# Adaptive average pooling: the last store issued by GpSimd instead of ScalarE

## The chip, the core and the metric

The kernel runs on one core of a Trainium2 chip. A core has five engines, each with an instruction queue of its own: TensorE (unused here), VectorE (DVE in the profile), ScalarE (ACT), GpSimd (POOL) and SyncE (SP). Sixteen DMA engines move data between the chip's main memory (DRAM) and the on-chip memory of 128 partitions. The metric is the device time of one execution in microseconds (us); lower is better.

## The reference

The input is x of shape 32 x 256 x 4096 in float32, the output has 256 values for each of the 8192 rows. Since 4096 / 256 = 16, every output is the mean of 16 neighbouring inputs:

```python
for i in range(output_size):
    start = int(i * length / output_size)
    end = int((i + 1) * length / output_size)
    result[:, :, i] = np.mean(x[:, :, start:end], axis=-1)
```

134.22 MB are read and 8.39 MB written, and each input is used once.

## The kernel before

The 8192 rows are taken as 16 tiles of 128 partitions by 4 rows, 64 KB for each partition and 8.39 MB in all. Fifteen tiles are loaded whole (L81, issued by SP) into two buffers named `xin` that take turns. The sixteenth tile is loaded in two halves (L89). All loads stand in SP's queue, and a load waits until the tile that used its buffer before has been reduced.

`pooled` (L62) reduces a tile. GpSimd adds the two halves of each window for the second half of the tile's windows, in place (L66). VectorE sums the windows of the first half, 16 wide (L69), and then the windows that GpSimd has shortened to 8 (L70). ScalarE multiplies the sums by 1/16 (L73). For the fifteen whole tiles the result goes into `res_many`, 60 KB for each partition, which stays on the chip until the end. For the sixteenth it goes into `res_last`, 4 KB for each partition.

There are three stores. All are issued by ScalarE, through the helper `store` (L57): `res_many` in one piece of 7680 KB once the fifteenth tile is done, and `res_last` after both of its halves, in two pieces of 120 and of 8 partitions (480 KB and 32 KB). The helper adds the name of each store to `tc.no_tile_sem_insts`, so that the closing code which the framework writes does not wait for the landing, and lets the store raise the semaphore `stored` by 16 when its data has landed.

The end of the program is written in this order. `tc.compile()` (L102) adds the closing code: every engine runs a DRAIN and signals, GpSimd gathers the signals and releases all, then GpSimd clears the framework's semaphores, and a second round of DRAIN, gathering and release follows. After that SP alone waits until `stored` is 48, three stores of 16 (L103), and clears it (L104); the profile shows the wait and the clear as one instruction on L104.

Of the kernel before, what the change touches and what calls it, by code (L numbers as in the profile page):

```python
# [1 line left out]

# [4 lines left out]


@with_exitstack
def kernel(  # L10
    ctx: ExitStack,
    tc: tile.TileContext,
    x: bass.AP,
    output_size: int,
    out: bass.AP,
):

    nc = tc.nc
    F32 = mybir.dt.float32
    X = mybir.AxisListType.X

    batch, channels, length = x.shape
    ob, oc, olen = out.shape
    assert ob == batch and oc == channels and olen == output_size
    assert length % output_size == 0
    window = length // output_size  # L30
    hw = window // 2
    inv_w = 1.0 / float(window)

    P = nc.NUM_PARTITIONS
    R = 4
    rows = batch * channels
    assert rows % (P * R) == 0
    ntiles = rows // (P * R)
    many = (ntiles - 1) * R
    cells = R * output_size  # L40
    m = cells // 2
    cols = R * length

    xr = x.rearrange("b c l -> (b c) l")
    orow = out.rearrange("b c o -> (b c) o")
    x_many = xr[0 : P * many, :].rearrange("(p r) l -> p (r l)", p=P, r=many)
    o_many = orow[0 : P * many, :].rearrange("(p r) o -> p (r o)", p=P, r=many)
    x_last = xr[P * many :, :].rearrange("(p r) l -> p (r l)", p=P, r=R)
    o_last = orow[P * many :, :].rearrange("(p r) o -> p (r o)", p=P, r=R)

    res_many = nc.alloc_sbuf_tensor("res_many", [P, (ntiles - 1) * cells], F32, align_bytes=256)
    res_last = nc.alloc_sbuf_tensor("res_last", [P, cells], F32, align_bytes=256)
    inpool = ctx.enter_context(tc.tile_pool(name="inpool", bufs=2))

    stored = nc.alloc_semaphore("stored")

    def store(out, in_):  # L57
        ins = nc.scalar.dma_start(out=out, in_=in_)
        tc.no_tile_sem_insts.add(ins.ins.name)
        ins.then_inc(stored, 16)  # L60

    def pooled(xin, res, base, n):  # L62


        k = n // 2
        nc.gpsimd.tensor_add(  # L66
            out=xin[:, k:n, 0:hw], in0=xin[:, k:n, 0:hw], in1=xin[:, k:n, hw:window]
        )
        nc.vector.reduce_sum(out=res[:, base : base + k], in_=xin[:, 0:k, :], axis=X)  # L69
        nc.vector.reduce_sum(  # L70
            out=res[:, base + k : base + n], in_=xin[:, k:n, 0:hw], axis=X
        )
        nc.scalar.mul(  # L73
            out=res[:, base : base + n], in_=res[:, base : base + n], mul=inv_w
        )

    for t in range(ntiles - 1):
        xbuf = inpool.tile([P, cols], F32, name="xin")
        if t == 1:
            nc.vector.memset(xbuf[:, 0:1536], 0.0)  # L80
        nc.sync.dma_start(out=xbuf, in_=x_many[:, t * cols : (t + 1) * cols])  # L81
        pooled(xbuf.rearrange("p (o w) -> p o w", w=window), res_many, t * cells, cells)

    half = cols // 2
    xbuf = inpool.tile([P, cols], F32, name="xin")
    for h in range(2):
        nc.sync.dma_start(  # L89
            out=xbuf[:, h * half : (h + 1) * half],  # L90
            in_=x_last[:, h * half : (h + 1) * half],
        )
    store(o_many, res_many[:, :])
    for h in range(2):
        xin = xbuf[:, h * half : (h + 1) * half].rearrange("p (o w) -> p o w", w=window)
        pooled(xin, res_last, h * m, m)
    for lo, hi in ((0, 120), (120, P)):
        store(o_last[lo:hi, :], res_last[lo:hi, :])

    ctx.pop_all().close()  # L100
    tc.close()
    tc.compile()  # L102
    nc.sync.wait_ge(stored, 48)  # L103
    nc.sync.sem_clear(stored)  # L104


# [1 line left out]
_INS = ['x', 'output_size']  # L108
_OUTS = [((32, 256, 256), 'float32')]

_NUMBERS = {'output_size': 256}


# [26 lines left out]
```

## Time and profile before

| | us |
|---|---|
| median of 3 runs (333.38 to 333.53) | 333.52 |
| the profiled execution's own time | 333.36 |
| its span, first to last instruction | 332.1 |
| DVE busy | 211.1 |
| POOL busy | 139.9 |
| ACT busy | 18.4 |

The profiled execution's time is 1.26 us more than its span, for what lies around the instructions. In the rows of the profile, q1 is the queue of DMAs that SP issues and q10 the queue of those that ACT issues. A name such as SPq or POOLq means the instruction queue of an engine: waits, DRAINs and issues of DMAs, none of which count as busy time. An issue of a DMA is short; its packets move later, on the sixteen DMA engines.

### The profile page before, as it was taken

What the parts mean: (1) busy time and instruction counts of PE and PEld (TensorE: products, weight loads), DVE (VectorE), ACT (ScalarE), POOL (GpSimd) and SP (SyncE); (2) the same over time, 40 slices, a digit from 0 to 9 for tenths busy, and PEclk for the clock granted to TensorE, in tenths of its full rate; (3) what the DMA queues carried; (4) which work ended last, traced back from release to release, by engine and by line L of the source; (5) the groups of instructions that cost most, each with busy time, mean ns of one, the idle gap of its engine ahead of it and who ended that gap; (6) DMA issues with size and microseconds to landing.
All of it is one profiled execution on the core that took longest, in us unless ns stands there. A gap on an engine that the chain in (4) does not pass through costs nothing.

```text
span 332.1 us, 167 instructions
## 1 busy us (share of the span) xinstructions
DVE 211.1 (64%) x35; ACT 18.4 (6%) x18; POOL 139.9 (42%) x21
## 2 busy tenths in 40 slices
DVE  1029396592939669293966929396693929569770
ACT  1000101001010100101010010101000010100100
POOL 0028091542809154270916427090642709068050
DMA  9898999989898998989899998989899898989997
GB/s 379 379 497 387 482 403 411 474 379 505 379 497 387 458 426 379 505 379 497 387 482 403 395 489 379 505 379 497 387 450 434 379 505 379 497 383 430 442 466 307
DMA packets 2743, 142.61 MB, mean 429 GB/s; under 512 B 311, under 2 KB 311, under 8 KB 439
## 3 DMA queue, kind: packets, MB, share of 16 engines
q1 hardware_dynamic: 2448, 134.22, 93.6%
q10 hardware_dynamic: 295, 8.39, 5.9%
HBM read 134.22 MB, written 8.39 MB: 429 GB/s over the span
## 4 chain that ended last, share of the span: by engine, by line
DMA 62%; POOL 20%; DVE 10%; issue 3%; POOLq 1%; ACT 0%
DMA xin<-in_x_dram 62%; POOL xin L66 20%; DVE res_many L70 9%; POOLq L102 1%; DVE res_last L70 1%; DVE xin L80 0%; ACT res_last L73 0%; POOLq L66 0%
## 5 line engine op out<-in xcount | busy, mean ns | idle before, releaser
L66 POOL TENSOR_TENSOR xin<-xin 128x4096 f32<-128x4096 f32 (+1 forms) x17 | 139.7, 8216 | 179.7 <-DMA xin<-in_x_dram 179.7
L69 DVE TENSOR_REDUCE res_many<-xin 128x512 f32<-128x8192 f32 x15 | 130.3, 8686 | 105.2 <-DMA xin<-in_x_dram 105.2
L70 DVE TENSOR_REDUCE res_many<-xin 128x512 f32<-128x4096 f32 x15 | 66.3, 4419 | 2.4 <-POOL xin L66 2.3
L73 ACT ACTIVATE res_many<-res_many 128x1024 f32<-128x1024 f32 x15 | 15.8, 1056 | 289.9 <-DVE res_many L70 289.9
L69 DVE TENSOR_REDUCE res_last<-xin 128x256 f32<-128x4096 f32 x2 | 8.8, 4414 | 2.1 <-DMA xin<-in_x_dram 2.1
L70 DVE TENSOR_REDUCE res_last<-xin 128x256 f32<-128x2048 f32 x2 | 4.6, 2280 | 0.1
L80 DVE MEMSET xin<- 128x1536 f32 x1 | 1.3, 1338 | 1.1 <-PEq L121 1.1
L73 ACT ACTIVATE res_last<-res_last 128x512 f32<-128x512 f32 x2 | 1.3, 629 | 13.7 <-DVE res_last L70 13.7
L73 ACT ACT_TABLE_LOAD x1 | 1.3, 1283 | 0.7 <-PEq L121 0.7
L121 POOL MEMSET const-float32-0.0<- 128x1 f32 x1 | 0.1, 98 | 0.2 <-issue 0.2
L121 POOL MEMSET const-bfloat16-1.0<- 128x1 bf16 x1 | 0.1, 101 | 0.0
L121 POOL MEMSET const-uint8-127<- 128x1 uint8 x1 | 0.1, 101 | 0.0
L121 POOL MEMSET const-float32-1.0<- 128x1 f32 x1 | 0.1, 98 | 0.0
## 6 DMA issues: line engine op xcount, KB each, us to landing
xin<-in_x_dram SPq DMA_DIRECT2D x2, 4096.0 KB, 21.6
out_dram<-res_many ACTq DMA_DIRECT2D x1, 7680.0 KB
out_dram<-res_last ACTq DMA_DIRECT2D x1, 480.0 KB
xin<-in_x_dram SPq DMA_DIRECT2D x15, 25.3
out_dram<-res_last ACTq DMA_DIRECT2D x1, 32.0 KB
```

Of the source, the lines that this page charges most:

```text
L66: nc.gpsimd.tensor_add(out=xin[:, k:n, 0:hw], in0=xin[:, k:n, 0:hw], in1=xin[:, k:n, hw:window])
L69: nc.vector.reduce_sum(out=res[:, base : base + k], in_=xin[:, 0:k, :], axis=X)
L70: nc.vector.reduce_sum(out=res[:, base + k : base + n], in_=xin[:, k:n, 0:hw], axis=X)
L73: nc.scalar.mul(out=res[:, base : base + n], in_=res[:, base : base + n], mul=inv_w)
L80: nc.vector.memset(xbuf[:, 0:1536], 0.0)
L102: tc.compile()
L121: nc = _bacc.Bacc("TRN2", target_bir_lowering=False, num_devices=1)
```

## The change

`store` gets the queue and the semaphore as arguments. The store of `res_many` stays with ScalarE and `stored`. The two stores of `res_last` are issued by GpSimd, after its own last work, and raise a new semaphore `stored_last`. At the end SP waits for 16 on `stored`, clears it, waits for 32 on `stored_last` and clears that.

```diff
     stored = nc.alloc_semaphore("stored")
+    stored_last = nc.alloc_semaphore("stored_last")
 
-    def store(out, in_):
-        ins = nc.scalar.dma_start(out=out, in_=in_)
+    def store(queue, sem, out, in_):
+        ins = queue.dma_start(out=out, in_=in_)
         tc.no_tile_sem_insts.add(ins.ins.name)
-        ins.then_inc(stored, 16)
+        ins.then_inc(sem, 16)
...
-    store(o_many, res_many[:, :])
+    store(nc.scalar, stored, o_many, res_many[:, :])
...
     for lo, hi in ((0, 120), (120, P)):
-        store(o_last[lo:hi, :], res_last[lo:hi, :])
+        store(nc.gpsimd, stored_last, o_last[lo:hi, :], res_last[lo:hi, :])
...
-    nc.sync.wait_ge(stored, 48)
+    nc.sync.wait_ge(stored, 16)
     nc.sync.sem_clear(stored)
+    nc.sync.wait_ge(stored_last, 32)
+    nc.sync.sem_clear(stored_last)
```

## The prediction, made before the changed kernel was run

> **What bounds the kernel now.** I read the page first, parts 1, 3 and 4.
>
> ```profile
> span 332.1 us, 167 instructions
> DVE 211.1 (64%) x35; ACT 18.4 (6%) x18; POOL 139.9 (42%) x21
> ...
> q1 hardware_dynamic: 2448, 134.22, 93.6%
> q10 hardware_dynamic: 295, 8.39, 5.9%
> HBM read 134.22 MB, written 8.39 MB: 429 GB/s over the span
> ```
>
> No engine is busy for more than 64%, while the packets of the two DMA queues fill 93.6 + 5.9 = 99.5% of the sixteen DMA engines' span. The kernel is bound by the bytes it moves. The change moves no byte less, so only the end can differ, where something may come after the last byte. The page's chain stops at the last multiply, so for the end I took the timeline of ACT from 300 us, and the waits of SP's queue.
>
> ```profile
> 306.69 1.06 ACT L73 ACTIVATE res_many<-res_many 128x1024 f32<-128x1024 f32 x1 [18.26 <-DVE res_many L70]
> 307.78 0.38 ACTq L58 DMA_DIRECT2D out_dram<-res_many  x1
> ...
> 322.12 0.63 ACT L73 ACTIVATE res_last<-res_last 128x512 f32<-128x512 f32 x1 [8.29 <-DVE res_last L70]
> 322.78 1.04 ACTq L58 DMA_DIRECT2D out_dram<-res_last  x2
> ...
> SPq L104 <- DMA out_dram<-res_last: 7.3, 1, 7.3
> ```
>
> The last multiply ends at 322.75, the two stores of `res_last` are issued from 322.78 to 323.82, and SP's last instruction waits 7.3 us for them, until 332.03. It is done at 332.06. What the 7.3 us are filled with is in the DMA view of three stretches, 314.1 to 315, 315 to 330 and 330 to 332.1 us, by the start of the packets:
>
> ```profile
> q10 hardware_dynamic: 16, 0.98, 251.9%
> q1 hardware_dynamic: 15, 0.00, 0.9%
> ...
> q10 hardware_dynamic: 96, 5.90, 90.7%
> ...
> DMA packets 167, 0.52 MB, mean 250 GB/s; under 512 B 39, under 2 KB 39, under 8 KB 167
> ```
>
> From 315 to 330 the engines do nothing but `res_many`: 96 packets in 0.907 x 15 x 16 = 217.7 engine-us, 2.27 us for each packet of 60 KB. Only then come the 128 packets of `res_last` and 39 small semaphore packets. The 8 or 9 data packets of an engine take about 1.4 us, and no packet starts after 331.6; the semaphore is full 0.43 us later. So `res_last`, issued at 323, has to queue until 330 anyway.
>
> The closing code is the last thing to read: L102 in narrow stretches around 324 us and the row of GpSimd's first DRAIN.
>
> ```profile
> L102 POOLq DRAIN  x1: 4556/4556/4556, 315.3 to 315.3; - x1
> ...
> L102 ACTq DRAIN  x1: 238/238/238, 323.9 to 323.9; - x1
> ...
> L102 SPq EVENT_SEMAPHORE  x1: 17/17/17, 324.7 to 324.7; - x1
> ```
>
> ACT's DRAIN (starting between 323.86 and 323.88) ends at 324.11, the last of the first round. SP's second release (starting between 324.73 and 324.75) ends at 324.76. The two rounds of gathering and release therefore take 0.65 us after the last DRAIN, all of it hidden under the 7.3 us in which `res_many` is still moving.
>
> **The change part by part.**
>
> *Taken off ACT.* Two issues, 1.04 us, and an ACT DRAIN that can be done about 1 us sooner. Nothing waits for that but the closing rounds, which have 7.3 us of cover: worth 0.
>
> *The wait on GpSimd.* The first store now waits in GpSimd's queue for the multiply at 322.75. GpSimd has had no work since its add ended at 319.77 (315.32 + 4.45). The hand-over costs 0.02 (DVE 322.10 to ACT 322.12) to 0.1 us. Behind the waiting store stand the second store, GpSimd's DRAIN and its gathering of the signals, and all engines wait for that gathering.
>
> *The issue on GpSimd.* No row shows one. From below there is ACT's issue of the same two stores, 0.43 to 0.58 us each (even 0.1 us, a GpSimd MEMSET, would gain nothing, since the DMA engines are taken until 330). From above there is GpSimd's longest single work nearby, 4.45 us each. I take 1 us each, near ACT's rows because the work is the same, more because another engine does it: issued by about 324.9. The first load, issued at 0.74, has its first packets after 1.72, so I add 1 us: 325.9. The cover is `res_many` until 330.02, so this costs 0. It would cost from an issue of the first store over 330.02 - 322.8 - 1.0 = 6.2 us on.
>
> *The transfer.* Same bytes, same engines, and a queue of its own. I expect the packets after those of `res_many`, or one of them between each two, since both give the same end. When `res_many` began (row of 314.1 to 315 above, and 16 q10 packets with 1 of q1 in the 2.25 us before), the load's sixteen semaphore packets on q1 were each let in after a single 60 KB packet of q10. So the engines seem to take turns packet by packet, and of the 8 packets for each engine at most 2 or 3 could slip in before `res_many` ends. All are done by 331.6 and landed by 332.02. Bounds: -0.15 us if the 9th packet of some engines finds a free one, +0.4 if the new queue's packets cost a quarter more. I take 0.
>
> *SP's end.* One wait and one clear more. SP's clear is 25 ns, and its closing instructions follow each other at 0.08 us (324.26, 324.35). After the closing code two of them cost 2 x (0.08 + 0.025) = 0.2 us if both semaphores are already full, where 0.04 us followed the landing before; if SP is already waiting, the second pair adds about 0.1.
>
> *GpSimd's DRAIN.* This decides. GpSimd's first DRAIN now stands behind its own two stores. Does it wait for their landing? The trace has a row on either side. ACT's DRAIN took 0.24 us, eight microseconds ahead of the landing of ACT's stores: by it the price is 0. GpSimd's DRAIN took 4.56 us, from 315.28 to 0.07 us after the add ended: by it a DRAIN of GpSimd is held by whatever GpSimd still owns. The nearest row for a GpSimd DRAIN is GpSimd's own, and the trace has one more hint: GpSimd's queue alone runs an INC_SWDGE_SEM at 0.1 us, by its name a count for DMAs, which no other queue shows. I take it that the DRAIN is held until `res_last` has landed. Then the closing rounds lose their cover and come behind the last byte:
>
> landing 332.02 + 0.07 (DRAIN) + 0.65 (two rounds) + 0.2 (SP) = 332.94, against 332.06 before: +0.88 us.
>
> The ends are 0.05 to 0.24 for the DRAIN, 0.6 to 0.7 for the rounds, 0.1 to 0.25 for SP and -0.15 to +0.4 for the transfer, together +0.56 to +1.55. The profiled execution would go from 333.36 to 334.24 and its span from 332.1 to 333.0; the runs' median is 0.16 above that execution, so 333.52 + 0.88 = 334.4.
>
> **The rivals.** 0.2% of 333.5 is 0.67 us, about what a measurement of this kernel can tell from no change.
>
> 1. *The DRAIN is not held* (the side of no change). It ends with the issue at about 325, the rounds at 325.7, under six more microseconds of cover, and only SP's second pair shows: +0.1 us, 333.6. For it: ACT's DRAIN. Against it: GpSimd's, 4.56 us. It decides unless GpSimd's DRAIN outlasts about 331.3, the landing less the rounds.
>
> 2. *Held, but `res_last` lands early.* If an engine gives the new queue one long turn, its 9 packets go after the `res_many` packet that runs at 325.9, by 328.2 + 1.4 = 329.6 at the latest, landed at 330.0, closing done at 330.8, still under `res_many`, which then lands at 332.0: +0.1 us, 333.6. The Trainium skill ("DMA: Bandwidth & Descriptors", Queues, rings and completion order) says so: an engine drains a whole packet, typically 9 to 17 descriptors, of one queue before it switches. By that rule the time would be 333.6; this trace speaks against it, with 16 q10 packets let in ahead of 15 of q1's.
>
> 3. *The issue is late.* With GpSimd's upper row, 4.45 us for each store, the second one is issued at 331.7 and moves from 332.7, landing at about 333.2, and with the DRAIN held the end is 334.1: +2.1 us, 335.6. Against it: ACT does the same in 0.5 us. The Trainium skill ("GPSIMD Engine Reference", Instruction dispatch) warns of about 6 us for the first call of freshly loaded code on GpSimd; as an estimate from it the packets would come at 322.8 + 6 + 2, 0.8 us after 330.02, and the time would be 335.2. No run here shows it for a DMA.
>
> 4. *Faster.* Were the packets spread evenly (-0.15) and the 0.43 us to the landing shared with `res_many`, the end could come 0.6 us sooner: 332.9. That is still inside 0.2%, and the packets' sum forbids more.
>
> **How the numbers follow.** Forecast 0.62; DRAIN not held 0.17; early landing 0.07; late issue 0.11; faster 0.03. Slower by over 0.2%: 0.58 of the forecast (its lowest ends fall below 0.67 us; I give them 0.04) + 0.11 = 0.69. Within 0.2%: 0.17 + 0.07 + 0.04 = 0.28. Faster by more needs something that I can't name: 0.03. The range reaches from 333.5, which takes in rivals 1 and 2 less the scatter of the runs, to 335.2, which takes in the forecast's own upper end (335.1) and part of rival 3. The forecast's own range is 334.1 to 335.1.
>
> **What would show it.** Right: a POOLq DRAIN on L102 several microseconds long, ending within 0.3 us of the last landing; the release on SP after it; SP's two clears at the very end, 0.7 to 0.9 us after the landing. The transfer step: still `res_many` alone until 330 and no packet of the new queue after 331.6. Wrong: GpSimd's DRAIN ending near 325 and SP waiting for `stored` at 331 (rival 1), the new queue's packets between 326 and 329 (rival 2), or a gap in the packets after 330 (rival 3).

## The result, and the profile after

The changed kernel takes 334.93 us (median of 4 runs, 334.89 to 335.0) against 333.52 us before (4 runs, 333.38 to 333.62): 1.41 us more, a ratio of 1.0043 with a 95% interval of 1.0029 to 1.0056. It is slower, as forecast, by more than the 0.88 us of the forecast and inside its range.

The page of the changed kernel shows the same work and the same bytes. GpSimd's row has two instructions and 1.2 us more, because the page counts GpSimd's issues of DMAs as work, which it does not do for ACT. GpSimd's queue appears as q0 with the kind software_dynamic:

```profile
span 333.2 us, 168 instructions
DVE 211.2 (63%) x35; ACT 18.4 (6%) x18; POOL 141.1 (42%) x23
...
q10 hardware_dynamic: 144, 7.86, 5.5%
q0 software_dynamic: 176, 0.52, 0.4%
```

The timeline of the end (start, duration, engine) shows GpSimd's two issues where ACT's stood, and the rows of the closing code (L104 here), in narrow stretches, show the DRAIN behind them. Columns of a row: count, shortest/median/longest in ns, first and last start.

```profile
322.08 0.63 ACT L74 ACTIVATE res_last<-res_last 128x512 f32<-128x512 f32 x1 [8.36 <-DVE res_last L71]
323.02 1.20 POOL L59 DMA_DIRECT2D out_dram<-res_last  x2 [3.29 <-ACT res_last L74]
...
L104 POOLq DRAIN  x1: 8947/8947/8947, 323.5 to 323.5; - x1
...
L104 SPq EVENT_SEMAPHORE  x1: 17/17/17, 333.0 to 333.0; - x1
...
L106 SPq EVENT_SEMAPHORE_RANGE_CLEAR  x1: 25/25/25, 333.1 to 333.1; - x1
...
L108 SPq EVENT_SEMAPHORE_RANGE_CLEAR  x1: 35/35/35, 333.2 to 333.2; - x1
```

The DRAIN on GpSimd starts at 323.46 and ends at 332.41. The last of the stores' semaphore increments in the trace is at 332.28. So the DRAIN was held until `res_last` had landed, and for 0.13 us more. (The row of the DRAIN starts before the second issue has ended, as that of before started just ahead of GpSimd's add; what counts is its end.) The release on SP, which stood at 324.74 before, is at 333.05, and SP's two clears end the program at 333.23. The row of SP's 7.3 us wait on L104 of before has no successor in the waits of SP's queue: when SP gets to its waits, both semaphores are full.

The stretches of the DMA view from 327.7 to 330 and from 331.6 on show the transfer:

```profile
q10 hardware_dynamic: 16, 0.98, 99.5%
q0 software_dynamic: 16, 0.06, 6.5%
...
DMA packets 17, 0.01 MB, mean 5 GB/s; under 512 B 15, under 2 KB 15, under 8 KB 17
```

While the sixteen last 60 KB packets of `res_many` start, sixteen packets of the new queue are let in, 0.06 MB: fifteen of 4 KB and one of a semaphore. The other 113 of 4 KB follow, and only 2 of them start after 331.6.

### The profile page after: what moved, and what is told of

The parts are those of the page before. It is cut to its first block, busy times and chain, and to the rows that moved or that the text cites. A ratio compares the mean times of both kernels' runs of the same rounds, so it can differ in the third digit from the quotient of the medians.

```text
span 333.2 us, 168 instructions
## 1 busy us (share of the span) xinstructions
DVE 211.2 (63%) x35; ACT 18.4 (6%) x18; POOL 141.1 (42%) x23
## 4 chain that ended last, share of the span: by engine, by line
DMA 66%; POOL 20%; DVE 10%; issue 1%; ACT 0%; POOLq 0%; SPq 0%
DMA xin<-in_x_dram 66%; POOL xin L67 20%; DVE res_many L71 9%; DVE res_last L71 1%; DVE xin L81 0%; POOL out_dram L59 0%; ACT res_last L74 0%; POOLq L104 0%; SPq L91 0%; POOLq L67 0%
## 5 line engine op out<-in xcount | busy, mean ns | idle before, releaser
L59 POOL DMA_DIRECT2D out_dram<-res_last x2 | 1.2, 606 | 3.3 <-ACT res_last L74 3.3
```

Source lines behind the costliest of these rows:

```text
L59: ins = queue.dma_start(out=out, in_=in_)
```

## The experiments

Two theories. **Cover**: GpSimd's DRAIN waits for the landing of GpSimd's own stores and so takes the closing code, and whatever else used to run under `res_many`, out of its cover. **Transfer** or **software queue**: the new queue's packets, or its use as such, cost the time. A smaller rival is the second **semaphore**. Medians are beside the kernel before on the same chip, 333.42 to 333.45 us.

**The semaphore alone.** ScalarE issues again, against the changed kernel:

```diff
-        store(nc.gpsimd, stored_last, o_last[lo:hi, :], res_last[lo:hi, :])
+        store(nc.scalar, stored_last, o_last[lo:hi, :], res_last[lo:hi, :])
```

> Only the second semaphore, with its wait and clear on SP; ScalarE issues all three stores as before. Theory 'cover' (the loss is GpSimd's DRAIN, which waits for the landing and pulls the closing code, and the other engines' end, behind it): +0.1 us against before, closing code at 324 us as before. Rival 'semaphore' (two waits and two clears at the end make the loss): +1.4 us as in the changed kernel. Rival 'transfer' (the packets of the software queue make the loss): +0.1 us.

333.43 us, ratio 0.9999 [0.9990, 1.0009]. The closing code's release is at 324.62 again. The second semaphore is not the cause.

**A queue of its own, but SP's.**

```diff
-        store(nc.gpsimd, stored_last, o_last[lo:hi, :], res_last[lo:hi, :])
+        store(nc.sync, stored_last, o_last[lo:hi, :], res_last[lo:hi, :])
```

> The stores of res_last in a queue of their own, but one that SP issues, with the own semaphore. Theory 'cover': SP's DRAIN is not held by a store of SP, as ACT's was not, so within 0.3 us of before (333.5 to 333.8). Rival 'transfer', in the form that any second queue beside res_many costs: about +1.4 us, 334.9.

333.52 us, ratio 1.0002 [0.9993, 1.0011]. The first packets of `res_last` go at 327.68, ahead of the end of `res_many` just as in the changed kernel. A second queue beside `res_many` costs nothing that can be measured. Nor is SP's DRAIN held by SP's own stores, whose last issue ends at 323.68 and which land at 332.05:

```profile
L104 SPq DRAIN  x2: 7/7/7, 324.0 to 324.1; - x2
```

**GpSimd's queue, used early.** GpSimd stores the first tile's results, ScalarE all else:

```diff
+        if t == 0:
+            store(nc.gpsimd, stored_last, o_many[:, 0:cells], res_many[:, 0:cells])
...
-    store(nc.scalar, stored, o_many, res_many[:, :])
+    store(nc.scalar, stored, o_many[:, cells:], res_many[:, cells:])
...
-        store(nc.gpsimd, stored_last, o_last[lo:hi, :], res_last[lo:hi, :])
+        store(nc.scalar, stored, o_last[lo:hi, :], res_last[lo:hi, :])
...
-    nc.sync.wait_ge(stored, 16)
+    nc.sync.wait_ge(stored, 48)
...
-    nc.sync.wait_ge(stored_last, 32)
+    nc.sync.wait_ge(stored_last, 16)
```

> GpSimd issues a 512 KB store with the own semaphore, but early: the first tile's part of res_many, after the first tile is scaled at about 37 us; ScalarE stores the other fourteen tiles and res_last at the end. Theory 'cover': the store has landed long before the end, GpSimd's closing DRAIN ends with its add at 320 us as before, so within 0.3 us of before. Rival 'software queue' (a program that uses GpSimd's queue pays for it at the end, wherever it is used): +0.4 to +1.4 us.

333.60 us, ratio 1.0004 [0.9996, 1.0013]. GpSimd's first DRAIN ends at 320.72, 0.16 us after its add. The use of the queue as such is not the cause.

**The wait for the landing, without GpSimd.** Against the kernel before:

```diff
-    stored = nc.alloc_semaphore("stored")
...
-        ins = nc.scalar.dma_start(out=out, in_=in_)
-        tc.no_tile_sem_insts.add(ins.ins.name)
-        ins.then_inc(stored, 16)
+        nc.scalar.dma_start(out=out, in_=in_)
...
-    nc.sync.wait_ge(stored, 48)
-    nc.sync.sem_clear(stored)
```

> All three stores issued by ScalarE as before, but the helper leaves the framework to wait for their landing ahead of its closing code; the semaphore stored and SP's wait and clear at the end fall away. No store of GpSimd at all. Theory 'cover': the closing rounds (0.65 us) and the 0.36 us that the changed kernel loses outside its span come behind the landing here too, less the clear: +0.8 to +1.2 us, 334.3 to 334.7. Rival 'transfer' or 'software queue': +0.0 to +0.1 us from the wait's place, at most the 0.65 us of the rounds with nothing outside the span.

334.85 us, ratio 1.0042 [1.0029, 1.0054]: the whole loss, with every store on ScalarE. It is a little above the range expected, on two counts: the release follows the landing by 0.94 us (332.07 to 333.01) where 0.65 was taken, since SP passes three more waits and two DRAINs of its own first (332.14 to 332.39), and the time outside the span is 1.77 us where 1.66 was taken, on which the last experiment bears. The rows of its closing code (L99) read like those of the changed kernel, except that GpSimd's DRAIN ends with its add and SP is the one that waits:

```profile
L99 POOLq EVENT_SEMAPHORE  x4: 17/17/17, 332.4 to 333.0; - x4
L99 POOLq DRAIN  x3: 34/83/4556, 314.9 to 332.8; - x3
L99 SPq DRAIN  x3: 7/7/7, 332.3 to 332.6; - x3
```

**GpSimd's two stores behind the closing code.** Against the changed kernel:

```diff
-    for lo, hi in ((0, 120), (120, P)):
-        store(nc.gpsimd, stored_last, o_last[lo:hi, :], res_last[lo:hi, :])
...
     tc.compile()
+    for lo, hi in ((0, 120), (120, P)):
+        nc.gpsimd.dma_start(out=o_last[lo:hi, :], in_=res_last[lo:hi, :]).then_inc(stored_last, 16)
```

> GpSimd issues the two stores of res_last behind the closing code instead of ahead of it, so that no DRAIN of the closing code stands behind them; everything else as in the changed kernel. Theory 'cover': closing code ends at about 323.5, the stores are issued by 325 and land at about 332.3, so only the later landing (0.26 us) and SP's second pair (0.1 us) remain: +0.3 to +0.4 us, 333.8 to 333.9; up to +0.5 more if what runs after the kernel's last instruction waits for GpSimd too. Rival 'transfer': +1.4 us as in the changed kernel, since the packets are the same.

333.46 us, ratio 1.0001 [0.9992, 1.0010]: the whole loss is gone, also the 0.3 to 0.4 us that were expected to remain, and the stores still are GpSimd's, with the same packets and the same semaphores. Its timeline of POOL, and its first DRAIN and last release on L102:

```profile
323.78 1.20 POOL L104 DMA_DIRECT2D out_dram<-res_last  x2 [4.24 <-POOLq L102]
...
L102 POOLq DRAIN  x1: 4554/4554/4554, 315.1 to 315.1; - x1
...
L102 SPq EVENT_SEMAPHORE  x1: 17/17/17, 323.2 to 323.2; - x1
```

The release comes at 323.18, and only then GpSimd issues. This and the run before it settle the cause from two sides: the loss comes without GpSimd's queue, and GpSimd's queue comes without the loss.

**Only the piece of 8 partitions by GpSimd.**

```diff
-    for lo, hi in ((0, 120), (120, P)):
-        store(nc.gpsimd, stored_last, o_last[lo:hi, :], res_last[lo:hi, :])
+    store(nc.scalar, stored, o_last[0:120, :], res_last[0:120, :])
+    store(nc.gpsimd, stored_last, o_last[120:P, :], res_last[120:P, :])
...
-    nc.sync.wait_ge(stored, 16)
+    nc.sync.wait_ge(stored, 32)
...
-    nc.sync.wait_ge(stored_last, 32)
+    nc.sync.wait_ge(stored_last, 16)
```

> GpSimd issues only the piece of 8 partitions (32 KB), ScalarE the 120. Theory 'cover': one small store holds GpSimd's DRAIN just as long, until about 332, so +1.1 to +1.4 us, 334.6 to 334.9. Rival 'transfer': a sixteenth of the bytes, so a small part of the loss, +0.1 to +0.2 us, 333.6 to 333.7.

333.68 us, ratio 1.0006 [0.9997, 1.0015]. The number expected was wrong, though the DRAIN is held, 8.58 us from 322.67 to 331.25:

```profile
L104 POOLq DRAIN  x1: 8582/8582/8582, 322.7 to 322.7; - x1
...
q10 hardware_dynamic: 96, 5.90, 90.9%
q0 software_dynamic: 16, 0.03, 0.6%
```

The sixteen packets of q0 in this stretch are the store's eight of 4 KB, which start from 327.7 to 327.9 ahead of the last sixteen of `res_many`, and eight small ones of the semaphore; sixteen more of the semaphore follow until 330.84, and the store is landed at 331.17. The closing code is done at 331.91, while ScalarE's 120 partitions land at 332.47. So a held DRAIN costs only what reaches past the last landing. This is the outcome of the prediction's second rival, on a store small enough for it, without a long turn of the new queue.

**The stores exchanged.** GpSimd issues `res_many`, ScalarE `res_last`:

```diff
-    store(nc.scalar, stored, o_many, res_many[:, :])
+    store(nc.gpsimd, stored, o_many, res_many[:, :])
...
-        store(nc.gpsimd, stored_last, o_last[lo:hi, :], res_last[lo:hi, :])
+        store(nc.scalar, stored_last, o_last[lo:hi, :], res_last[lo:hi, :])
```

> The other way round: GpSimd issues res_many (at about 308 us), ScalarE issues res_last. GpSimd's own add of the last half tile comes after the issue. Theory 'cover': the DRAIN is held until res_many has landed, about 331 to 332, so +0.8 to +1.4 us, 334.3 to 334.9, although the last store is ScalarE's again. Rival 'transfer of the last store': +0.1 us.

333.70 us, ratio 1.0012 [1.0003, 1.0021]; again less than expected. The DRAIN lasts 16.20 us, from 315.18 to 331.38, 0.08 us after the landing of `res_many` at 331.30; it is held by a store issued 7 us before it:

```profile
L104 POOLq DRAIN  x1: 16199/16199/16199, 315.2 to 315.2; - x1
```

The release is at 332.03 and the last landing at 332.41: the closing code lies just under the last landing.

**One piece of 128 partitions, and the changed kernel again.**

```diff
-    for lo, hi in ((0, 120), (120, P)):
-        store(nc.gpsimd, stored_last, o_last[lo:hi, :], res_last[lo:hi, :])
+    store(nc.gpsimd, stored_last, o_last, res_last[:, :])
...
-    nc.sync.wait_ge(stored_last, 32)
+    nc.sync.wait_ge(stored_last, 16)
```

> As the changed kernel, but one store of 128 partitions instead of 120 and 8. Theory: DRAIN held to the landing as before the split was undone, +1.1 to +1.4 us; the question is the landing, 332.28 in the changed kernel against 332.02 before. If the later landing comes from how the two pieces fall on the DMA engines (some engines get 9 or 10 packets), it should come back to about 332.0 here; if it is the software queue's packets as such, it stays at 332.3.

334.60 us, ratio 1.0034 [1.0022, 1.0047]; the last landing is at 332.04. That fitted the split as the reason for the later landing, so the changed kernel was run once more, with two kernels that store one piece of 128 partitions, by ScalarE, and by GpSimd behind the closing code:

> The changed kernel once more, beside the three below. Theory 'cover': the DRAIN ends about 0.1 us after the last landing, the closing code's release 0.65 us later, +1.2 to +1.5 us against before. Whether the landing (332.28 in the first profile of it, 332.02 in that of before) is really later: if it is scatter of single executions it can come out anywhere between 332.0 and 332.5 here.

> ScalarE issues res_last in one piece of 128 partitions, with the own semaphore. Both theories: the same as before within 0.3 us (333.2 to 333.8). If the split into 120 and 8 partitions lengthens the transfer, it is up to 0.2 us faster than before.

> GpSimd issues res_last in one piece of 128 partitions behind the closing code. Theory 'cover': no DRAIN stands behind the store, so the same as before within 0.3 us (333.2 to 333.8), and 1.2 to 1.5 us faster than the changed kernel. If the software queue's packets as such land later, +0.2 to +0.4 us against before.

The changed kernel: 334.79 us, ratio 1.0041 [1.0028, 1.0055], and this time its last landing is at 332.05, with the split as it was. ScalarE's single piece: 333.54, 1.0002 [0.9993, 1.0011], landing 332.19. GpSimd's single piece behind the closing code: 333.55, 1.0003 [0.9994, 1.0012], landing 332.31. The later landing of the first profile was scatter. None of the variants beats the kernel before.

**The time outside the span.** In the profiled execution of the changed kernel the time is 334.89 and the last instruction ends at 333.23: 1.66 us outside the span, where before had 1.30 (333.36 less 332.06; the 1.26 given for it above comes from the span rounded up to 332.1). The traces so far, times in us; "release on SP" is the start of SP's last release by the closing code:

| kernel | last landing | first POOL DRAIN ends | release on SP | SP's end | own time | release + 1.84 | SP's end + 1.30 |
|---|---|---|---|---|---|---|---|
| before | 332.02 | 319.84 | 324.74 | 332.06 | 333.36 | 326.58 | 333.36 |
| changed | 332.28 | 332.41 | 333.05 | 333.23 | 334.89 | 334.89 | 334.53 |
| changed, again | 332.05 | 332.18 | 332.82 | 333.01 | 334.66 | 334.66 | 334.31 |
| wait in the closing code | 332.07 | 319.49 | 333.01 | 333.03 | 334.85 | 334.85 | 334.33 |
| 8 partitions by GpSimd | 332.47 | 331.25 | 331.89 | 332.59 | 333.88 | 333.73 | 333.89 |
| stores exchanged | 332.41 | 331.38 | 332.03 | 332.46 | 333.87 | 333.87 | 333.76 |
| behind the closing code | 332.23 | 319.61 | 323.18 | 332.29 | 333.58 | 325.02 | 333.59 |

The own time is the larger of the last two columns, to 0.01 us. The two constants were read off these traces; the last run tests the rule, by adding work on SP after the release:

```diff
     nc.sync.sem_clear(stored)
+    nc.sync.sem_clear(stored)
+    nc.sync.sem_clear(stored)
+    nc.sync.sem_clear(stored)
+    nc.sync.sem_clear(stored)
```

> The changed kernel with four more clears of the semaphore stored on SP, after its first clear: some 0.3 us more work on SP between the closing code's last release and SP's last instruction. In the profiled executions so far the time is the larger of two sums, the release on SP + 1.84 us and the end of SP's last instruction + 1.30 us. By that rule SP's end moves by about 0.3 us but the time does not: the profiled execution comes 1.84 us after its release and its time less its span falls from 1.66 to about 1.4 us; the median stays at 334.8 to 334.9. Rival 'in series' (SP's clears add to the end, as the prediction's sum had it): the time stays 1.66 us longer than the span, and the median rises to about 335.1 to 335.2.

334.94 us, ratio 1.0043 [1.0029, 1.0057]. In its profiled execution the release is at 332.90, SP ends 0.41 us after it at 333.31, and the time is 334.74, again the release + 1.84; 1.43 us lie outside the span. The median is 0.04 us above the 334.9 expected, against the 335.1 to 335.2 of the rival. Its six clears, from L106 to L112, are hidden:

```profile
L106 SPq EVENT_SEMAPHORE_RANGE_CLEAR  x1: 25/25/25, 333.0 to 333.0; - x1
...
L112 SPq EVENT_SEMAPHORE_RANGE_CLEAR  x1: 30/30/30, 333.3 to 333.3; - x1
```

The rule held. The other executions say the same, to the 0.1 us to which their spans are known: 1.61 to 1.71 us outside the span in all nine of the changed kernel, 1.25 to 1.36 us in every one of the kernel before, 1.38 to 1.46 us in all five with the four clears. So by the rule something after the closing code takes 1.84 us from the release on, and only its last 1.30 us wait for SP. The trace has a hint of what: increments of semaphore 2, which the kernel does not use. Before, four of them fall between 325.0 and 325.3, right after the release, and the rest after SP's end; in the changed kernel all fall after SP's end. With GpSimd's stores behind the closing code two come at 323.48 and 323.51, right after the release, and the next two only at 325.50 and 325.54, after GpSimd's issues have ended at 324.98. That the engines hand over to each other there is argued from these events, not shown.

## Why the prediction was right, step by step

*What bounds the kernel: right.* `res_many` filled the DMA engines to 330 in both kernels, and nothing the change did before that is seen in the time.

*The wait and the issue on GpSimd: cost 0, as forecast.* The hand-over from ScalarE took 0.30 us (322.72 to 323.02), not 0.02 to 0.1, and the issues took 0.70 and 0.51 us instead of the 1 us assumed. Seven microseconds of cover took both. Rival 3 falls: no issue of GpSimd's took the 6 us of freshly loaded code that the Trainium skill ("GPSIMD Engine Reference", Instruction dispatch) warns of; the first DMA it issued, here and at 37 us in the early store, took 0.70 us.

*The transfer: 0, as forecast.* The last landing in six profiles whose `res_last` was issued by GpSimd lies between 332.04 and 332.31, and in six without a store of GpSimd at the end between 332.02 and 332.31; only the kernel of the 8 partitions and the one of the exchanged stores land later, at 332.47 and 332.41 in one profile each, and why stays open. The step said that engines would take turns packet by packet, with 2 or 3 packets slipping in at most for each engine; fifteen of 128 did, on average about one for each. The sign given for this step still failed: `res_many` was not alone until 330, and seventeen packets of the new queue, two of them data, started after 331.6. The size of the step was right all the same, as the landing did not move. The long turns of the Trainium skill ("DMA: Bandwidth & Descriptors", Queues, rings and completion order), 9 to 17 descriptors, did not show; by that rule the time would have been 333.6.

*GpSimd's DRAIN: right, and the step that decides.* It ended 0.13 us after the last landing (0.07 taken; 0.08 to 0.13 in all six profiles where it was held). Rival 1 is out.

*The two rounds: right.* 0.64 us from the DRAIN's end to the start of SP's release (332.41 to 333.05), 0.65 taken to its end.

*SP's end: mis-sized, and this is where the 0.88 us came out short.* SP's two clears took 0.18 us after the release, near the 0.2 of the sum, and the program ended 0.95 us after the landing, where 0.7 to 0.9 was the sign. But the sum then carried the time outside the span over unchanged, as if it were a constant. In fact the end of the execution follows the release by 1.84 us, SP's clears lying beside that; by the rule above, 0.54 us of these (1.84 less 1.30) were under `res_many` too before the change. With the table's terms, for an equal landing:

- before, 0.04 + 1.30 = 1.34 us from the landing to the end of the execution;
- after, 0.13 + 0.64 + 1.84 = 2.61 us.

That is a loss of 1.27 us where the sum had 0.88. Of the 0.39 us between them, 0.36 lie outside the span (1.66 against 1.30) and 0.06 in the DRAIN (0.13 against 0.07); SP and the rounds gave back 0.03. The second profile of the changed kernel, with its landing at 332.05, shows nearly that: 334.66 - 333.36 = 1.30 us. The first has 0.26 us of landing scatter besides: 1.53 us. The medians, +1.41 and +1.35 us, lie between. That +1.41 us still fell within the +0.56 to +1.55 of the sum is in part luck: the room came from the 0.4 us allowed for the transfer, without which the upper end is +1.15 and which the transfer did not take, while the term that grew had no bounds at all. By the same figures a held DRAIN begins to cost, as an estimate, when it ends after 332.06 + 1.30 - 1.84 - 0.64 = 330.88, not after the 331.3 that rival 1 named.

## What to carry to other kernels

Before a store at the end is moved to another engine's queue, look at what follows it in that queue: here a DRAIN on GpSimd was held by GpSimd's own stores, for 8.58 to 16.20 us, and one on ScalarE (0.24 us) or SP (7 ns) was not. What a hold costs is read from the later of two ends, that of the closing code after the DRAIN with what follows it, and that of the last landing, so a small store that lands early holds for nothing. Closing work that lies under a last transfer costs its whole length once it loses that cover, also the part after the kernel's last instruction: here the time less the span gave it away.

## What the runs showed of the hardware that was not expected

- The time outside the span is not a constant: 1.30 us where the engines were released early, 1.66 and 1.77 us where the release came last, 1.41 and 1.43 us where the two ends lay close together.
- GpSimd's DRAIN is held by a store that has not landed, also one issued 7 us earlier: 16.20 us behind `res_many`, against 0.24 us for ScalarE's DRAIN behind stores that had 8 us to go.
- Issuing a store took GpSimd 0.70 us for 120 or 128 partitions and 0.51 us for 8 behind it, not far from ScalarE's 0.29 to 0.70 us for the same two pieces.
